# First gate's vectors moved out of the start, three scales summed on VectorE, adaLN loads issued from GpSimd's queue

## The chip, the cores and the metric

The kernel runs on one core of one Trainium2 chip. The metric is the device time of the whole program in microseconds (us), from the launch of its first instruction to its last. The kernel before took 2820.3 us, the median of three runs (2819.34 to 2823.11).

In the profile the engines are PE (TensorE's matmuls), PEld (TensorE's weight loads), DVE (VectorE), ACT (ScalarE), POOL (GpSimd) and SP (SyncE, which only issues DMAs). A name with q, as SPq, is the engine's sequencer, where DMA issues and waits stand. L250 is line 250 of the kernel.

## The reference, cut to what matters

Two layers over 512 latent and 256 context tokens of width 1024. A layer is a half-step SwiGLU of width 2816, a token mixer (layer 0: differential attention, layer 1: windowed attention with grouped queries), and a second half-step SwiGLU. Each of the three sub-layers is normalised, then shifted and scaled, and its result goes through a gate. These nine vectors of 1024 (shift, scale, gate, three times) come from one product per layer (adaLN):

```python
mod_l = silu(c) @ ada_w[i] + ada_b[i]         # for latent tokens
mod_c = silu(c_ctx) @ ada_w[i] + ada_b[i]     # for context tokens
sh1, sc1, g1, sh2, sc2, g2, sh3, sc3, g3 = split(mod_l, 9)
x = x + 0.5 * g1 * swiglu(rms(x) * (1 + sc1) + sh1, pre_wi, pre_wo)
```

`ada_w` is 1024 x 9216 float32 per layer. Everything is float32; the large products are done as three products of split operands (hi x hi, lo x hi, hi x lo).

## The kernel before, in words

**Layout.** `x` stays on the chip, features on the 128 partitions in 8 chunks (k or d, 0 to 7), 768 tokens along a row. An adaLN vector m (0 to 8; m = 0 is the first shift, 1 the first scale, 2 the first gate) has 8 chunks too, for the two types of token.

**How an adaLN vector is made.** There are three ways. `vector_job(m, k)` loads a row block of 128 x 1024 of `ada_w` (512 KB, tag `araw`, nine buffers) and multiplies it on VectorE with the replicated `crep = silu(c)`, once per type, each product summing along its row (L190); then it adds the bias (L191) and, for m = 2, halves it (L193). `scale_job(k)` makes chunk k of the scale on TensorE: eight pairs of small matmuls against `cvec` (L205), a turn (L209), and the bias plus 1 on VectorE (L211). `Halves` does the same as `vector_job` in half rows: a job loads 128 x 512 (256 KB, tag `wh`, three buffers), two products on VectorE (L250), and after eight chunks GpSimd adds the sums to `mod`, which already holds the bias (L229, L227), in L254; two halves q make a vector, and m = 2 or 8 is halved at the end (L256). One step is one job; `beside` runs steps after the up step of each f of the FFN, none up to f = 3 and one per f from there, `between` runs 13 of 16 (or 10) blocks' worth inside each down step.

**The start.** The 22 f of the FFN are 128 columns each of gate and up. f = 0 is fed: `feed(k)` normalises chunk k (L1156), applies shift and scale on ScalarE (L1159), splits it into `h_h` (L1160) and `h_l` (L1161), and TensorE multiplies that chunk at once (L537). `feed(k)` also issues the loads of the vector job m = 0 and the scale job of chunk k + 2 and runs the sums made ready two chunks earlier. After up(0), `beside(0)` runs the eight vector jobs of m = 2 and then releases the pool `start`. f = 1 and 2 are plain (L537) and f = 1 also makes the sums for the fast form; from f = 3 on `Seven.up` (L470) does an up step with seven products in place of eight. After f = 4, 8, ... a down step follows (L584), whose results go through the gate into `x` on VectorE (L396); the first of these needs vector m = 2 complete.

**What sets the order.** The program is written in one order; a planner simulates the engines and queues and orders each engine's instructions, so that work may move ahead of its place where its inputs are there. What is marked `keep` stays in program order on its queue. Nearly all loads stand in SP's queue: weights (`raw`, three buffers, L97), and the kept loads of `ada_w` (L184, L247) and of c (L236). An engine and a queue work in order: a load that waits for its buffer holds up what stands behind it.

**On GpSimd.** It adds squares for the next norm during the last down step and the output projection (L343), takes powers (L300, L627), does part of the attention's rotation (L648, L651), and the sums of adaLN (L254).

Of the kernel before, what the change touches and what calls it, by code (L numbers as in the profile page):

```python
# [12 lines left out]
ALU = mybir.AluOpType  # L13
# [4 lines left out]
P = 128  # L18
D = 1024
KC = D // P  # L20
# [11 lines left out]
def halves_of(nt):  # L32

    return [(0, SEQ, 0, (0, 1)), (SEQ, CTX, 1, (2,))] if nt == T else parts_of(nt)
# [8 lines left out]
def hybrid_backbone_kernel(ctx: ExitStack, tc: tile.TileContext, I, out):  # L43
    nc = tc.nc
# [9 lines left out]
    def one(name, tag="one"):  # L54
        return ps1.tile([P, 512], F32, name=name, tag=tag)
# [14 lines left out]
    keep = tc.keep_in_program_order  # L70
# [53 lines left out]
    adab = const.tile([P, 2, NMOD * KC], F32, name="adab")  # L124
# [56 lines left out]
    def vector_job(m, k, pool, crep, bufs):  # L181

        w = pool.tile([P, D], F32, name="araw", tag="araw", bufs=bufs)
        keep(nc.sync.dma_start(w, I["ada_w"][0, m * KC + k]))  # L184
        md = mods[0][m][2][:, :, k]

        def sums():
            for ty in range(2):
                o = w if ty else pool.tile([P, D], BF16, name="junk", tag="junk", bufs=2)
                nc.vector.scalar_tensor_tensor(o, w, 1.0, crep[:, ty], ALU.mult, ALU.mult, accum_out=md[:, ty:ty + 1])  # L190
            nc.vector.tensor_add(md, md, adab[:, 0, m * KC + k:m * KC + k + 1].broadcast_to([P, 2]))  # L191
            if m == 2:
                nc.vector.tensor_scalar_mul(md, md, 0.5)  # L193
        return sums

    def scale_job(k, pool, bufs):


        w = pool.tile([P, D], F32, name="araw", tag="araw", bufs=bufs)
        keep(nc.sync.dma_start(w, I["ada_s"][k]))  # L200

        def sums():
            ps = one("ps_a", "acc")
            for i in range(KC):
                nc.tensor.matmul(ps[:2, :P], cvec[:, i], w[:, i * P:(i + 1) * P], start=i == 0, stop=i == KC - 1)  # L205
            row = pool.tile([2, P], F32, name="row", tag="row", bufs=2)
            nc.scalar.copy(row, ps[:2, :P])
            pt = one("ps_b", "acc")[:, :2]
            nc.tensor.matmul(pt, row, ident[:2, :2], start=True, stop=True)  # L209
            bias = adab[:, 0, KC + k:KC + k + 1].broadcast_to([P, 2])  # L210
            nc.vector.scalar_tensor_tensor(mods[0][1][2][:, :, k], pt, 1.0, bias, ALU.add, ALU.add)  # L211
        return sums

    class Halves:
# [6 lines left out]
        def add(self, l, ms):  # L221
            def bias(m):
                md = const.tile([P, 2, KC], F32, name=f"mod{l}_{m}")
                mods[l][m] = md[:, 0], md[:, 1], md
                b = adab[:, l, m * KC:(m + 1) * KC].unsqueeze(1).broadcast_to([P, 2, KC])
                if m in (1, 4, 7):
                    nc.gpsimd.tensor_scalar_add(md, b, 1.0)  # L227
                else:
                    nc.gpsimd.tensor_copy(md, b)  # L229

            def silu(room, q):
                cs = []
                for nm in ("c", "c_ctx"):
                    pool, tag, bufs = (small, "ar", 3) if room[1] == "wh" else room
                    t = pool.tile([P, 512], F32, name="ch", tag=tag, bufs=bufs)
                    keep(nc.sync.dma_start(t, I[nm][q * 512:(q + 1) * 512].partition_broadcast(P)))  # L236
                    nc.scalar.activation(t, t, AF.Silu)
                    cs.append(t)
                self.c = cs

            def job(room, q, m, d):
                types = (0, 1) if l == 0 or m < 5 else (0,)
                if d == 0:
                    self.part = small.tile([P, 2, KC], F32, name="part", tag="part", bufs=2)
                pool, tag, bufs = room
                w = pool.tile([P, 512], F32, name="wh", tag=tag, bufs=bufs)
                keep(nc.sync.dma_start(w, I["ada_w"][l, m * KC + d, :, q * 512:(q + 1) * 512]))  # L247
                for ty in types:
                    o = w if ty == types[-1] else small.tile([P, 512], BF16, name="junkh", tag="tmp", bufs=4)
                    nc.vector.scalar_tensor_tensor(o, w, 1.0, self.c[ty], ALU.mult, ALU.mult,  # L250
                                                   accum_out=self.part[:, ty, d:d + 1])
                if d == KC - 1:
                    md, n = mods[l][m][2], len(types)
                    nc.gpsimd.tensor_add(md[:, :n], md[:, :n], self.part[:, :n])  # L254
                    if q == 1 and m in (2, 8):
                        nc.gpsimd.tensor_scalar_mul(md[:, :n], md[:, :n], 0.5)  # L256

            for q in range(2):
                for m in ms:
                    for d in range(KC):  # L260
                        def f(room, q=q, m=m, d=d):
                            if q == 0 and d == 0:
                                bias(m)
                            if m == ms[0] and d == 0:
                                silu(room, q)
                            job(room, q, m, d)
                        self.steps.append(f)
# [842 lines left out]
        return box["o"]  # L1110

    all_ = halves_of(T)
    FIRST = 9
    halves = Halves()
    h0 = Norm(0, 0, T, "right", "h0_")
    h0.open()
# [1 line left out]
    start = start_cm.__enter__()  # L1118
    cvec = start.tile([P, KC, 2], F32, name="cvec")
    nc.sync.dma_start(cvec, I["cvec"])  # L1120
    nc.scalar.activation(cvec, cvec, AF.Silu)
    for m in range(3):
        md = const.tile([P, 2, KC], F32, name=f"mod0_{m}")
        mods[0][m] = md[:, 0], md[:, 1], md
    with tc.tile_pool(name="f0", bufs=1) as pool:
        load_small()
        load_x(all_[0])
        crep = ada_vectors(start)
        load_x(all_[1])
        keep(nc.sync.dma_start(adab, I["ada_b"]))  # L1130
        first = [(vector_job(0, k, start, crep, FIRST), scale_job(k, start, FIRST)) for k in range(2)]
        xr = [pool.tile([P, T], F32, name="xr", tag=("ah", "al")[d % 2], bufs=5) for d in range(KC)]
        rall = pool.tile([P, T], F32, name="rall", tag="ah", bufs=5)
        steps = []
        for s0, n, _, _ in all_:
            tk = slice(s0, s0 + n)
            for d in range(KC):
                nc.scalar.activation(xr[d][:, s0:s0 + n], x[:, d, s0:s0 + n], AF.Square)
            for step in (1, 2, 4):
                for d in range(0, KC, 2 * step):  # L1140
                    nc.vector.tensor_add(xr[d][:, s0:s0 + n], xr[d][:, s0:s0 + n], xr[d + step][:, s0:s0 + n])
            steps.append(rstd_steps(xr[0][:, tk], n, D, lambda pr, _, tk=tk: nc.scalar.copy(rall[:, tk], pr), pool))
        for z in zip(*steps):
            for step in z:
                step()
        for z in first:
            for f in z:
                f()
        later = {}

        def feed(k):

            if k + 2 < KC:
                later[k + 2] = [vector_job(0, k + 2, start, crep, FIRST), scale_job(k + 2, start, FIRST)]
            hi, lo = h0.reg.hi[:, k], h0.reg.lo[:, k]
            nc.vector.tensor_mul(xr[k], x[:, k], rall)  # L1156
            for s0, n, ty, _ in all_:
                sh, sc = (mods[0][i][ty][:, k:k + 1] for i in range(2))
                nc.scalar.activation(xr[k][:, s0:s0 + n], xr[k][:, s0:s0 + n], AF.Identity, bias=sh, scale=sc)  # L1159
            nc.scalar.copy(hi, xr[k])  # L1160
            nc.vector.tensor_sub(lo, xr[k], hi.bitcast(F32))  # L1161
            for f in later.get(k + 2, ()):
                f()
        h1 = Norm(0, 3, T, "right", "h1_")

        def up_done():
            h0.reg.close()
            h1.open()
        halves.add(0, range(3, NMOD - 1))
        others = halves.beside(3)  # L1170

        def beside(f, seven):
            if f == 0:
                for k in range(KC):
                    vector_job(2, k, start, crep, FIRST)()
                start_cm.__exit__(None, None, None)
            else:
                if f == 17:
                    load_gains(0, "a")
                    load_rest(small)  # L1180
                if f < NF - 1:
                    others(f, seven)
        ffn(0, 0, I["pre_wi"][0], I["pre_wo"][0], T, h0, pool, up_done, h1.follow, "right", beside, halves.between(13), feed, xr)
# [125 lines left out]
```

## Time and profile before

| | |
|---|---|
| median of 3 runs | 2820.3 us (2819.34 to 2823.11) |
| the profiled execution: time, span | 2823.49 us, 2821.3 us |
| granted TensorE clock, mean | 0.988 |
| TensorE, VectorE, ScalarE, GpSimd busy | 96%, 77%, 43%, 12% |
| HBM read | 256 MB, 93 GB/s over the span |

The span is the time from the first to the last instruction of one profiled execution; its parts are read against its own time. A busy share is a mean over stages with different limits. The granted clock is the share of full TensorE speed; below 1 the engine ran part of the stretch at the lower of its two levels.

### The profile page before, as it was taken

How to read it: one execution, taken by the hardware profiler on the slowest of the kernel's cores; microseconds unless marked ns; L12 is line 12 of the kernel's file. 1: busy time of each engine (PE TensorE's matmuls, PEld its weight loads, DVE VectorE, ACT ScalarE, POOL GpSimd, SP SyncE). 2: the span in 40 equal slices, each digit the busy share in tenths (PEclk: the TensorE clock that was granted, in tenths of full speed). 3: DMA queues.
4: the chain of work that ended last, by engine and by line, in shares of the span. 5: the costliest groups of instructions: out<-in, count | busy, mean ns of one | idle time of the engine just before them, and what ended most of it. 6: DMA issues, size and time to landing. Idle time of an engine off the chain costs nothing. (4 is left out here: it accounts for less than half of the span.)

```text
span 2821.3 us, 47391 instructions
## 1 busy us (share of the span) xinstructions
PE 2705.1 (96%) x18028; PEld 2565.6 (91%) x18028; DVE 2176.2 (77%) x4703; ACT 1205.7 (43%) x2995; POOL 339.3 (12%) x464
## 2 busy tenths in 40 slices
PE   6899999999999899999999999999999999999999
PEld 4799998899999878999899989999999999999999
DVE  8788887876867768877787697777777766588887
ACT  4433332355656644333233352333235666444443
POOL 1000000034533421000000100000003421100000
PEclk9999999999999999999999999999999999999999
DMA  7234433321101142332333223433332101233232
GB/s 278 82 109 127 138 98 111 107 105 46 31 31 31 42 134 63 120 113 78 116 120 102 63 64 124 135 123 95 124 115 93 46 16 38 68 98 100 96 98 97
DMA packets 97555, 266.48 MB, mean 94 GB/s; under 512 B 12464, under 2 KB 16560, under 8 KB 97200
## 3 DMA queue, kind: packets, MB, share of 16 engines
q1 hardware_dynamic: 90816, 251.78, 27.6%
q10 hardware_dynamic: 6512, 11.68, 1.3%
q8 instruction: 142, 2.33, 0.3%
q14 instruction: 85, 0.70, 0.1%
HBM read 256.07 MB, written 7.34 MB: 93 GB/s over the span
## 5 line engine op out<-in xcount | busy, mean ns | idle before, releaser
L73 ACT CAST whi<-raw 128x512 fp32r<-128x512 f32 x548 | 336.1, 620 | 650.6 <-PE ps_dn L584 291.8
L584 PE MATMUL ps_dn<-ah,whi 128*128 128x256 f32 (+1 forms) x1456 | 464.9, 322 | 11.7 <-DVE x L396 9.5
L584 PE MATMUL ps_dn<-al,whi 128*128 128x256 f32 (+1 forms) x1456 | 462.2, 320 | 0.1
L584 PE MATMUL ps_dn<-ah,wlo 128*128 128x256 f32 (+1 forms) x1456 | 455.1, 319 | 1.1 <-DVE wlo L74 1.0
L74 DVE TENSOR_TENSOR wlo<-raw,whi 128x512 fp32r<-128x512 f32 x548 | 378.2, 695 | 65.5 <-ACT whi L73 49.9
L470 PE MATMUL ps_up<-h_h,whi 128*128 128x384 f32 (+1 forms) x1216 | 394.6, 325 | 8.3 <-DVE u L497 6.3
L470 PE MATMUL ps_up<-h_h,wlo 128*128 128x384 f32 (+1 forms) x1216 | 392.2, 324 | 0.7 <-DVE wlo L74 0.7
L470 PE MATMUL ps_up<-h_l,whi 128*128 128x384 f32 (+1 forms) x1216 | 392.5, 323 | 0.0
L396 DVE SCALAR_TENSOR_TENSOR x<-ps_dn,mod,x 128x256 f32<-128x256 f32 (+1 forms) x442 | 241.0, 556 | 126.6 <-PE ps_dn L584 103.0
L584 PEld LDWEIGHTS ps_dn<-ah,whi 128*128 128x128 f32 x1456 | 276.6, 191 | 35.8 <-ACT whi L73 8.5
L73 ACT CAST whi<-s 128x512 fp32r<-128x512 f32 x304 | 188.3, 620 | 266.6 <-PE ps_up L470 220.4
L584 PEld LDWEIGHTS ps_dn<-ah,wlo 128*128 128x128 f32 x1456 | 276.4, 191 | 21.8 <-DVE wlo L74 2.0
L584 PEld LDWEIGHTS ps_dn<-al,whi 128*128 128x128 f32 x1456 | 277.8, 191 | 19.6 <-DVE al L74 0.3
L470 PEld LDWEIGHTS ps_up<-h_h,whi 128*128 128x128 f32 x1216 | 229.0, 188 | 14.0 <-DVE u L497 8.9
L74 DVE TENSOR_TENSOR wlo<-s,whi 128x512 fp32r<-128x512 f32 x304 | 208.5, 687 | 31.4 <-ACT whi L73 27.7
L470 PEld LDWEIGHTS ps_up<-h_h,wlo 128*128 128x128 f32 x1216 | 228.3, 188 | 2.8 <-DVE wlo L74 2.3
L470 PEld LDWEIGHTS ps_up<-h_l,whi 128*128 128x128 f32 x1216 | 228.9, 188 | 0.5
L254 POOL TENSOR_TENSOR mod<-mod,part 128x16 f32<-128x16 f32 (+1 forms) x30 | 13.2, 439 | 1428.6 <-DVE wh L250 1428.6
L673 PE MATMUL ps_qkv<-whi,h_h 128*128 128x256 f32 x608 | 177.8, 292 | 3.2 <-DVE a L629 2.2
L250 DVE SCALAR_TENSOR_TENSOR wh<-wh,ch 128x512 f32<-128x512 f32 x240 | 163.4, 693 | 18.3 <-DMA wh<-in_ada_w 18.2
L673 PE MATMUL ps_qkv<-wlo,h_h 128*128 128x256 f32 x608 | 174.1, 286 | 0.7 <-DVE wlo L74 0.7
L673 PE MATMUL ps_qkv<-whi,h_l 128*128 128x256 f32 x608 | 173.6, 286 | 0.0
(236 smaller groups left out, 6536.5 us busy)
## 6 DMA issues: line engine op xcount, KB each, us to landing
wh<-in_ada_w SPq DMA_DIRECT2D x240, 256.0 KB, 3.8
raw<-in_pre_wi SPq DMA_DIRECT2D x88, 512.0 KB, 3.5
raw<-in_post_wi SPq DMA_DIRECT2D x88, 512.0 KB, 3.5
raw<-in_pre_wo SPq DMA_DIRECT2D x44, 512.0 KB, 3.6
raw<-in_post_wo SPq DMA_DIRECT2D x44, 512.0 KB, 3.6
araw<-in_ada_w SPq DMA_DIRECT2D x16, 512.0 KB, 4.4
raw<-in_a_w_qk SPq DMA_DIRECT2D x16, 512.0 KB, 3.5
araw<-in_ada_s SPq DMA_DIRECT2D x8, 512.0 KB, 10.0
```

Source lines behind the costliest of these rows:

```text
L73: nc.scalar.copy(hi, src)
L74: nc.vector.tensor_sub(lo, src, hi.bitcast(F32))
L250: nc.vector.scalar_tensor_tensor(o, w, 1.0, self.c[ty], ALU.mult, ALU.mult, accum_out=self.part[:, ty, d:d + 1])
L254: nc.gpsimd.tensor_add(md[:, :n], md[:, :n], self.part[:, :n])
L396: nc.vector.scalar_tensor_tensor(x[:, d, s0:s0 + n], ps, gate[ty][:, d:d + 1], x[:, d, s0:s0 + n], ALU.mult, ALU.add)
L470: nc.tensor.matmul(ps, ww, z[:, k, :n], start=first and k == 0 and i == 0, stop=k == 3 and i == 2, skip_group_check=True)
L584: nc.tensor.matmul(ps, wv, a[:, s0:s0 + n], start=fi == 0 and k == 0, stop=fi == nf - 1 and k == 2)
L673: nc.tensor.matmul(ps, h[:, k, bt], w, start=n == 0, stop=n == 23)
```

## The change

The vector jobs of m = 2 leave `beside(0)`. The gate's vector becomes the first member of `Halves` (16 steps, with c's two vectors loaded again for it), and `beside` runs 0, 4 and 12 steps after up(1), up(2) and up(3). Of the eight scale chunks, k = 5, 6, 7 are made by `vector_job(1, k)` in place of `scale_job`. The loads of `Halves` (`wh` and `ch`, in both layers) are issued from GpSimd's queue, not SP's.

```diff
-            nc.vector.tensor_add(md, md, adab[:, 0, m * KC + k:m * KC + k + 1].broadcast_to([P, 2]))
-            if m == 2:
-                nc.vector.tensor_scalar_mul(md, md, 0.5)
+            bias = adab[:, 0, m * KC + k:m * KC + k + 1].broadcast_to([P, 2])
+            if m:
+                nc.vector.scalar_tensor_tensor(md, md, 1.0, bias, ALU.add, ALU.add)
+            else:
+                nc.vector.tensor_add(md, md, bias)
...
-                    keep(nc.sync.dma_start(t, I[nm][q * 512:(q + 1) * 512].partition_broadcast(P)))
+                    keep(nc.gpsimd.dma_start(t, I[nm][q * 512:(q + 1) * 512].partition_broadcast(P)))
...
-                keep(nc.sync.dma_start(w, I["ada_w"][l, m * KC + d, :, q * 512:(q + 1) * 512]))
+                keep(nc.gpsimd.dma_start(w, I["ada_w"][l, m * KC + d, :, q * 512:(q + 1) * 512]))
...
-    FIRST = 9
+    FIRST, ONPE = 9, 5
...
-    for m in range(3):
+    for m in range(2):
...
-                later[k + 2] = [vector_job(0, k + 2, start, crep, FIRST), scale_job(k + 2, start, FIRST)]
+                later[k + 2] = [vector_job(0, k + 2, start, crep, FIRST),
+                                scale_job(k + 2, start, FIRST) if k + 2 < ONPE else
+                                vector_job(1, k + 2, start, crep, FIRST)]
...
+        halves.add(0, (2,))
         halves.add(0, range(3, NMOD - 1))
-        others = halves.beside(3)
+        others = halves.beside(3, (0, 4, 12))
...
             if f == 0:
-                for k in range(KC):
-                    vector_job(2, k, start, crep, FIRST)()
                 start_cm.__exit__(None, None, None)
```

## Rows read from the trace of the kernel before

**Rows 1.** The page, part 1: busy time (share of the span) x instructions.
```profile
PE 2705.1 (96%) x18028; PEld 2565.6 (91%) x18028; DVE 2176.2 (77%) x4703; ACT 1205.7 (43%) x2995; POOL 339.3 (12%) x464
```
**Rows 2.** Windows: stretch, length, busy per engine (x instructions), clock, DMA share, GB/s.
```profile
35.00:81.00 46.00, 30.57 (x179) 22.82 (x176) 46.00 (x101) 18.05 (x32) 0.00 (x0) 0.93 0.44 155
81.00:102.00 21.00, 20.29 (x97) 17.14 (x98) 18.30 (x37) 9.74 (x21) 0.00 (x0) 0.83 0.25 76
102.00:119.00 17.00, 17.00 (x99) 14.80 (x98) 7.00 (x13) 5.68 (x12) 0.00 (x0) 1.00 0.09 31
119.00:156.00 37.00, 36.25 (x206) 35.00 (x205) 33.03 (x79) 14.27 (x28) 0.53 (x1) 1.00 0.53 172
```
**Rows 3.** Timeline of TensorE: start, duration, what, count [idle before <- releaser].
```profile
74.11 0.28 PE L537 MATMUL ps_up<-h_h,wlo 128*128 128x256 f32 x1
80.92 0.79 PE L537 MATMUL ps_up<-h_h,whi 128*128 128x512 f32 x1 [6.54 <-ACT whi L73]
...
101.84 0.39 PE L537 MATMUL ps_up<-h_h,whi 128*128 128x512 f32 x1
...
118.73 0.34 PE L470 MATMUL ps_up<-h_h,whi 128*128 128x384 f32 x1
```
**Rows 4.** Timeline of VectorE, 71 to 77 us.
```profile
71.71 0.95 DVE L1161 TENSOR_TENSOR h_l<-xr,h_h 128x768 fp32r<-128x768 f32 x1
...
76.30 0.68 DVE L570 TENSOR_TENSOR sg<-sg,ps_up 128x512 f32<-128x512 f32 x1
```
**Rows 5.** Timeline of ScalarE, 73 to 81 us.
```profile
73.48 1.09 ACT L569 ACTIVATE sg<-ps_up 128x512 f32<-128x512 f32 x2 [5.28 <-PE ps_up L537]
77.01 0.62 ACT L73 CAST ah<-sg 128x512 fp32r<-128x512 f32 x1 [2.44 <-DVE sg L570]
...
80.25 1.14 ACT L73 CAST whi<-raw 128x512 fp32r<-128x512 f32 x2
```
**Rows 6.** Groups by line, 0 to 200 us: count | busy, mean ns | idle before.
```profile
L205 PE MATMUL ps_a<-araw,cvec 128*2 128x128 f32 x128 | 20.4, 326 | 6.5 <-DVE mod L211 3.8 <-DMA araw<-in_ada_s 2.8
L190 DVE SCALAR_TENSOR_TENSOR junk<-araw,crep 128x1024 bf16<-128x1024 f32 x16 | 19.5, 1218 | 0.0
```
**Rows 7.** Timeline of VectorE, 127 to 157 us.
```profile
127.22 0.69 DVE L250 SCALAR_TENSOR_TENSOR junkh<-wh,ch 128x512 bf16<-128x512 f32 x1
...
150.49 0.69 DVE L250 SCALAR_TENSOR_TENSOR wh<-wh,ch 128x512 f32<-128x512 f32 x1
...
151.10 0.69 DVE L250 SCALAR_TENSOR_TENSOR wh<-wh,ch 128x512 f32<-128x512 f32 x1
...
156.04 0.75 DVE L396 SCALAR_TENSOR_TENSOR x<-ps_dn,mod,x 128x512 f32<-128x512 f32 x1
```
**Rows 8.** Windows of L190 alone: VectorE busy (x instructions, reads of the accumulator counted), clock, DMA.
```profile
35.00:72.70 37.70, 27.33 (x47) 0.95 0.53 189
72.70:81.00 8.30, 4.70 (x8) 0.82 0.00 0
```
**Rows 9.** Waits of TensorE, 95 to 420 us: us in total, times, longest.
```profile
PE ps_dn L584 <- DVE x L396: 3.2, 1, 3.2
PE ps_dn L584 <- DVE wlo L74: 0.7, 1, 0.7
PE ps_up L470 <- DVE u L491: 0.4, 2, 0.2
```
**Rows 10.** Waits of GpSimd, whole span.
```profile
POOL mod L254 <- DVE wh L250: 1428.6, 30, 124.0
```
**Rows 11.** DMA issues: queue, count, KB each, median us to landing.
```profile
wh<-in_ada_w SPq DMA_DIRECT2D x240, 256.0 KB, 3.8
```
**Rows 12.** Waits of VectorE, whole span.
```profile
DVE s L456 <- DMA raw<-in_pre_wi: 38.4, 31, 2.9
...
DVE wh L250 <- DMA wh<-in_ada_w: 18.2, 18, 2.3
...
DVE junkh L250 <- DMA wh<-in_ada_w: 16.4, 19, 1.9
```

## The prediction

> **What bounds the kernel now.** First I read the page's busy shares: TensorE is busy 96% of the span [rows 1]. So only TensorE's idle stretches can be won, about 116 us in all (2821.3 minus 2705.1), and most of the change must be judged by whether it touches one of them. The table of windows then shows where they lie near the edit [rows 2]: from 35 to 81 us TensorE is busy 30.57 of 46.00 us while VectorE is busy for all 46.00. The start is bound by VectorE. From 81 to 102 us TensorE is busy nearly throughout but its granted clock is 0.83; from 102 us on it is busy at full clock, and VectorE has room (7.00 of 17.00 us, then 33.03 of 37.00). The waits of TensorE from 95 to 420 us say the same: all three together are 4.3 us, none of them for a DMA [rows 9]. So the pre-FFN of layer 0 is bound by VectorE up to 81 us and by TensorE afterwards.
>
> How the start ends is read in order of time. VectorE finishes the last `h_l` (L1161) at 72.66 us [rows 4], TensorE's last product of f=0 stands at 74.11 us, and the first of f=1 at 80.92 us, after 6.54 us idle put down to the cast of `whi` on ScalarE [rows 3]. ScalarE had taken the two SiLUs at 73.48, then waited 2.44 us for VectorE's `sg`, and only cast `whi` at 80.25 [rows 5]. VectorE delivered `sg` (L570) at 76.30 us, because it was still summing gate vectors [rows 4].
>
> **The change, part by part.** *Gate vectors leave the start.* A product of L190 with its read of the accumulator costs 1.18 us (4.70 us for the four pairs from 72.7 to 81 us, [rows 8]). In 35 to 81 us stand 27.33 + 4.70 = 32.03 us of them, so 27 of the 32 that the program has (16 for the first vector, 16 for the gate; the count is x16 for each of the two shapes, the first of them in [rows 6]). Five were done before. Left are therefore 11 products of the first vector, and the edit adds two for each of k = 5, 6, 7 of the scale, 6 in all. Of the 23 products that now lie ahead of the last `h_l`, 17 remain: 6 x 1.18 = 7.1 us less VectorE time before it. The bounds are 0 (if the loads and ScalarE set the pace at once) and 7.1 us; I take 6, near the upper end, since VectorE has no idle time there at all [rows 2], less about 1 us because the last product must still pass through ScalarE before the last `h_l`.
>
> *Three scales move from TensorE to VectorE.* The 6 products above are their price. On TensorE the 128 matmuls of L205 are 20.4 us for eight chunks [rows 6], 2.55 us each, so 7.7 us is freed; TensorE has 15.4 us idle in that stretch [rows 2], so I cost this at nothing. The cover is VectorE being later than TensorE; without it the 7.7 us would be a gain on top.
>
> *The passage from f=0 to f=1.* Four more gate products, the x8 of [rows 8], vanish from beside `sg`. If ScalarE keeps its order (SiLU, `ah`, `whi`), `sg` can follow the SiLU at 74.6 on the old time scale instead of at 76.30, and both casts of `ah` then run one after the other; `whi` comes at about 76.4 in place of 80.25, a gain of 3.9 us. If `whi` is cast right after the SiLU, the gain is 5.7. I take 4.5. What is late next is the release of f=0's `whi` buffers by TensorE, which no edit touches.
>
> *The clock.* f=2 takes 118.73 - 101.84 = 16.89 us, f=1 101.84 - 80.92 = 20.92 us for the same 96 matmuls [rows 3], and the granted clock is 0.83 over f=1 [rows 2], so part of it ran at 1.2 instead of 2.4 GHz, after TensorE had stood idle for 6.54 us. With a gap of 1 to 3 us the 4.0 us may come back wholly, partly or not at all; I take 2, the middle.
>
> *The gate comes back in f=2 and f=3.* 16 half rows, two products each of 0.61 us (150.49 to 151.10 us to the next, [rows 7]): 19.5 us of VectorE, needed before the first `x` of the down step, now at 156.04 us [rows 7]. VectorE's idle time from 81 to 156 us is 2.7 + 10.0 + 4.0 = 16.7 us [rows 2], and in that stretch some eleven half rows of later vectors are already done ahead of that `x`, the first at 127.22 us [rows 7]; they carry no date there and can slide behind. So the cost is between nothing and 19.5 - 4.0 = 15.5 us (if only the idle time behind 119 us can be used, because the gate's half rows are issued behind up(2) and up(3)). I take 2, near the lower end, because the first half rows now are done some 30 us ahead of their place in the program.
>
> *Loads from GpSimd's queue.* 256 issues (16 of them the silu vectors' loads) leave SP's queue, and 16 for the gate join them on GpSimd's. TensorE waits for no weight load in [rows 9], so SP's relief is worth nothing by itself; VectorE's 38.4 us until `raw` [rows 12] is idle time of an engine that has some. On GpSimd the loads stand in one queue with the sums `mod` (L254), which wait for the last product of a vector [rows 10]: behind each of 32 such sums the next vector's first load goes out late. No row shows a load issued by GpSimd. From [rows 11] one lands 3.8 us after its issue from SP. Bounds: a gain of 4 us (all the waits of [rows 9]) and, per sum, a loss of 3.8 us less what TensorE has in hand. A half slab feeds 12 matmuls of 0.176 us (16.89 / 96), 2.1 us; that leaves 1.7 us for each of 32, 54 us at most. I take 0, as the row it is nearest to is VectorE's waiting for these loads now, 18.2 + 16.4 us over the two shapes of L250 [rows 12], of which TensorE's 4.3 us show no trace.
>
> A rule speaks against this part. The large VectorE instructions of this stretch take two inputs and all run at one pace (512 columns in 0.69 us, 1024 in 1.22 us, [rows 6, 7]); none shows a doubled rate. The Trainium skill, page "SBUF — State Buffer", section "SBUF: two separate sides", says that a DMA issued from GpSimd has its descriptors written by GpSimd's cores, and that these are locked out while VectorE runs an instruction that takes both ports. No such instruction stands among those rows, so by the rule, too, the sum is the one above; but it is a reason to keep the chance of late loads above nothing.
>
> *Sum.* 6 + 4.5 + 2 - 2 + 0 = 10.5 us less. The profiled execution's span was 2821.3 us and its time 2823.49, 2.2 us around it; the median of the runs is 2820.3, 3.2 us below. From span 2821.3 to 2810.8; the execution 2813.0; the median 2809.8, say 2810.
>
> **Rivals.** (a) *The gate takes it back.* VectorE becomes the bound in f=2 to f=4: with 15.5 us in place of 2 the sum is 12.5 - 15.5, so 2823. For it: VectorE is busy 33 of 37 us from 119 to 156. Against it: 10 us idle just before, and the eleven half rows that can slide. 0.12.
> (b) *Loads behind the sums on GpSimd's queue come late*, place: the 32 sums L254 from layer 0's pre-FFN to layer 1's; price 1.7 us each on TensorE once VectorE waits for a half row in front of a `wlo`. From 7 such places on it eats the gain (10.5 / 1.7 = 6.2), at half of them (16 x 1.7 = 27 us) the time is 2837, at all 2864. For it: 1428.6 us of GpSimd's idle time are spent ahead of exactly these sums [rows 10]. Against it: three buffers of `wh`, and much of that waiting lies where no vector is due soon. 0.13.
> (c) *SP's relief gains as well*: weights land earlier, VectorE's 38.4 us until `raw` shrinks, the clock's 4 us come back wholly. 2 + 3 us more: 2805. For it: VectorE is at 80 to 90% beside TensorE's work. Against it: [rows 9] names no load. 0.11.
> (d) *The start does not get shorter as reckoned*, because the scales' six products or the loads set the pace; then only the passage is won, 4.5 - 2 = 2.5 us: 2818. For it: the scales put 7.1 us on the engine that is the bound. Against it: 12 gate products leave the same place. 0.07.
> The forecast has 0.57.
>
> **How the numbers follow.** The time is the forecast's, 2810. What this kernel's measurement can tell from no change is about 0.2%, 5.6 us: faster is under 2814.7, slower over 2825.9. Faster: the forecast but for a little (0.55) and (c), 0.66. Same: the rest of the forecast, (d) and most of (a), 0.17. Slower: (b) and the tail of (a), 0.17. The range reaches down to 2802 (passage 5.7, start 7.1, clock 4.0, with 1 us of (c)) and up to 2824 so that it holds (d) and most of (a), and leaves out (b).
>
> **What would show it.** In the profile after: the last `h_l` at 65 to 68 us; the first product of f=1 at 69 to 72 us with under 3 us idle before it; granted clock over f=1 above 0.9; first `x` of the down step at 142 to 148 us; L250 products from 85 us on; TensorE's waits from 95 to 420 us still a few us. Wrong would be: `x` (L396) later than 150 us (then (a)), or waits of VectorE for `wh` well over the 34.6 us of now, with TensorE waiting for `wlo` behind them (then (b)).

## The result, and the profile after

The changed kernel takes 2868.03 us (median of 4 runs, 2864.5 to 2870.53), the kernel before beside it 2821.49 us: a ratio of 1.0158, 95% interval [1.0145, 1.0171]. It is 46.5 us slower where 10 us faster was forecast. Two single executions of later runs, one of the six with the gate alone and one of the eight with the split 2, 6, 8, took 5406 and 5280 us, and the ratios leave them out. In the program after, the lines behind L190 stand two further on (L1161 four, as L1165): the products of the half rows are L252 (before L250), their loads L249, the sums into `mod` L256, the up step of the fast form L472, the down step L586, `x` L398.

The start went as forecast. From VectorE's timeline the last `h_l` and the first `x` of the down step, 4.3 and 8.4 us ahead of [rows 4, 7]:

```profile
67.37 0.95 DVE L1165 TENSOR_TENSOR h_l<-xr,h_h 128x768 fp32r<-128x768 f32 x1
...
147.65 0.74 DVE L398 SCALAR_TENSOR_TENSOR x<-ps_dn,mod,x 128x512 f32<-128x512 f32 x1
```

In TensorE's timeline the last product of f=0 and the first of f=1 follow each other with no idle time in brackets; before, 6.54 us stood here [rows 3]:

```profile
69.77 0.29 PE L539 MATMUL ps_up<-h_h,wlo 128*128 128x256 f32 x1
69.90 0.40 PE L539 MATMUL ps_up<-h_h,whi 128*128 128x512 f32 x1
```

Two of the prediction's signs did not come: the products of half rows begin at 70.85 us and not at 85, and TensorE's waits from 95 to 420 us, 4.3 us before [rows 9], are 20.5 us.

The windows answer to [rows 2] with its columns (stretch, length, PE, PEld, DVE, ACT, POOL busy, clock, DMA share, GB/s). The first four are its stretches, the last three lie further on:

```profile
35.00:81.00 46.00, 36.52 (x183) 29.28 (x182) 46.00 (x94) 25.14 (x45) 2.28 (x4) 0.89 0.34 117
81.00:102.00 21.00, 21.00 (x119) 18.16 (x119) 19.91 (x48) 6.21 (x13) 2.78 (x6) 1.00 0.32 102
102.00:119.00 17.00, 14.18 (x84) 13.86 (x83) 13.80 (x31) 8.58 (x18) 4.52 (x9) 0.97 0.52 163
119.00:156.00 37.00, 34.95 (x190) 32.34 (x190) 33.49 (x83) 11.47 (x21) 6.73 (x14) 0.97 0.53 167
160.00:260.00 100.00, 91.81 (x514) 86.38 (x513) 94.75 (x230) 30.61 (x55) 20.04 (x39) 0.98 0.46 146
1100.00:1200.00 100.00, 80.91 (x469) 74.41 (x469) 95.61 (x228) 38.31 (x78) 16.94 (x32) 0.91 0.37 118
1700.00:1800.00 100.00, 89.18 (x487) 82.07 (x486) 87.14 (x205) 30.02 (x57) 26.21 (x50) 0.95 0.50 163
```

The last three of before:

```profile
160.00:260.00 100.00, 99.85 (x572) 94.30 (x571) 87.14 (x193) 32.70 (x59) 0.76 (x2) 1.00 0.37 118
1100.00:1200.00 100.00, 97.53 (x573) 89.58 (x572) 90.32 (x190) 41.24 (x81) 0.22 (x1) 1.00 0.31 101
1700.00:1800.00 100.00, 99.36 (x564) 94.14 (x563) 78.74 (x166) 33.74 (x63) 1.19 (x2) 1.00 0.38 122
```

From 81 to 102 us TensorE is fully busy at full clock (before 0.83). What is lost is lost later: 8, 17 and 10 us of TensorE in the last three windows, while VectorE is busier than before. They lie in the early up and down steps of layer 0's first FFN, of its second one, and of layer 1's first. The page and the waits of VectorE and GpSimd (us in total, times, longest) show whether the half rows came late:

```profile
PE 2710.9 (95%) x17974; PEld 2575.9 (90%) x17974; DVE 2191.6 (76%) x4731; ACT 1206.8 (42%) x2996; POOL 483.3 (17%) x744
...
L249 POOL DMA_DIRECT2D wh<-in_ada_w x256 | 138.7, 543 | 684.0 <-DVE wh L252 633.8
...
wh<-in_ada_w POOLq DMA_DIRECT2D x256, 256.0 KB, 3.3
```
```profile
POOL wh L249 <- DVE wh L252: 633.8, 162, 163.6
POOL mod L256 <- DVE wh L252: 146.1, 30, 10.0
...
DVE junkh L252 <- DMA wh<-in_ada_w: 18.4, 19, 2.3
...
DVE wh L252 <- DMA wh<-in_ada_w: 10.0, 11, 4.4
```

They did not. VectorE waits 28.4 us for `wh` in all, less than the 34.6 us of [rows 12]. GpSimd's loads wait almost only for VectorE to empty a buffer of `wh`. The sums wait 146.1 us where they waited 1428.6 [rows 10], but much of that has only changed its place: GpSimd now spends 684.0 us idle ahead of the loads, in the same stream. The products of the half rows alone (DVE busy, clock, DMA share, GB/s), after and then before:

```profile
60.00:160.00 100.00, 32.50 (x96) 0.97 0.43 137
160.00:260.00 100.00, 42.79 (x128) 0.98 0.46 146
260.00:360.00 100.00, 33.82 (x100) 0.97 0.41 137
360.00:460.00 100.00, 0.00 (x0) 1.00 0.21 70
```
```profile
60.00:160.00 100.00, 15.24 (x46) 0.95 0.33 109
160.00:260.00 100.00, 26.24 (x78) 1.00 0.37 118
260.00:360.00 100.00, 24.15 (x72) 1.00 0.36 117
360.00:460.00 100.00, 21.49 (x64) 1.00 0.34 110
```

Before, the half rows were spread evenly, from 160 us on at 21 to 26 us in 100. After, they crowd into the first 300 us of the FFN and are used up by 360 us.

The costliest place shows how that stops TensorE. First windows of all engines (columns as above), then of L252 alone:

```profile
1120.00:1140.00 20.00, 19.77 (x111) 17.14 (x110) 20.00 (x45) 6.57 (x13) 2.68 (x5) 1.00 0.43 132
1140.00:1160.00 20.00, 14.54 (x90) 13.04 (x88) 20.00 (x49) 8.12 (x18) 3.11 (x6) 0.97 0.33 105
1160.00:1180.00 20.00, 10.18 (x42) 10.16 (x43) 19.70 (x50) 5.95 (x11) 4.85 (x9) 0.60 0.41 132
```
```profile
1120.00:1140.00 20.00, 6.67 (x20) 1.00 0.43 132
1140.00:1160.00 20.00, 6.71 (x20) 0.97 0.33 105
1160.00:1180.00 20.00, 9.94 (x30) 0.60 0.41 132
```

VectorE has no idle time from 1120 to 1160 us; 13.4 of the 40 us are products of half rows, for vectors of later stages. Timelines of VectorE, then ScalarE, then TensorE at the end of it (start, duration, what, [idle before <- releaser]):

```profile
1162.30 0.68 DVE L458 TENSOR_TENSOR s<-raw 128x512 f32<-128x512 f32 x1
1162.91 0.68 DVE L252 SCALAR_TENSOR_TENSOR wh<-wh,ch 128x512 f32<-128x512 f32 x1
...
1165.54 0.68 DVE L459 TENSOR_TENSOR s<-s,raw 128x512 f32<-128x512 f32 x1
1166.14 0.68 DVE L252 SCALAR_TENSOR_TENSOR junkh<-wh,ch 128x512 bf16<-128x512 f32 x1
...
1166.75 0.68 DVE L460 TENSOR_TENSOR s<-raw 128x512 f32<-128x512 f32 x1
...
1167.82 0.68 DVE L252 SCALAR_TENSOR_TENSOR junkh<-wh,ch 128x512 bf16<-128x512 f32 x1
...
1168.43 0.68 DVE L461 TENSOR_TENSOR s<-raw,s 128x512 f32<-128x512 f32 x1
```
```profile
1169.15 0.62 ACT L73 CAST whi<-s 128x512 fp32r<-128x512 f32 x1 [4.54 <-DVE s L461]
```
```profile
1169.82 0.69 PE L472 MATMUL ps_up<-h_h,whi 128*128 128x384 f32 x1 [15.28 <-ACT whi L73]
```

TensorE's wait reads "for ScalarE". ScalarE had nothing to do for 4.54 us, because the sums `s` of the fast form's weights came one by one from VectorE, with a product of a half row between each pair. Eight such products, some 5.4 us, stand in TensorE's 15.28 us of idleness; that the rest of it is work that had piled up behind the earlier ones is argued and not shown. The granted clock from 1160 to 1180 us, with the end of the 15.28 us of idleness in it, is 0.60.

### The profile page after: what moved, and what is told of

It reads as the page before. It is cut to its first block, busy times and chain, and to the rows that moved or that the text cites. A ratio compares the mean times of both kernels' runs of the same rounds, so it can differ in the third digit from the quotient of the medians.

```text
span 2866.0 us, 47437 instructions
## 1 busy us (share of the span) xinstructions
PE 2710.9 (95%) x17974; PEld 2575.9 (90%) x17974; DVE 2191.6 (76%) x4731; ACT 1206.8 (42%) x2996; POOL 483.3 (17%) x744
## 4 chain that ended last, share of the span: by engine, by line
PE 73%; DVE 12%; issue 5%; DMA 4%; ACT 3%; POOL 3%; SPq 0%; ACTq 0%; POOLq 0%; DVEq 0%
PE ps_up L472 28%; PE ps_dn L586 21%; PE ps_qkv L675 8%; PE ps_up L539 4%; PE ps_dn L752 3%; DVE wlo L74 2%; PE ps_av L1021 2%; DMA wh<-in_ada_w 2%; DVE wh L252 1%; DVE junkh L252 1%; PE ps_av L854 1%; PE ps_s L810 1%; PE ps_qkvs L688 1%; PE ps_pt L1010 1%; DMA raw<-in_pre_wi 1%
## 5 line engine op out<-in xcount | busy, mean ns | idle before, releaser
L586 PE MATMUL ps_dn<-ah,whi 128*128 128x256 f32 (+1 forms) x1456 | 464.3, 322 | 11.3 <-DVE x L398 9.0
L586 PE MATMUL ps_dn<-al,whi 128*128 128x256 f32 (+1 forms) x1456 | 462.5, 320 | 0.1
L586 PE MATMUL ps_dn<-ah,wlo 128*128 128x256 f32 (+1 forms) x1456 | 454.0, 319 | 2.0 <-DVE wlo L74 2.0
L472 PE MATMUL ps_up<-h_h,whi 128*128 128x384 f32 (+1 forms) x1216 | 399.7, 329 | 25.4 <-ACT whi L73 20.4
L472 PE MATMUL ps_up<-h_l,whi 128*128 128x384 f32 (+1 forms) x1216 | 397.7, 327 | 0.0
L472 PE MATMUL ps_up<-h_h,wlo 128*128 128x384 f32 (+1 forms) x1216 | 395.8, 327 | 1.6 <-DVE wlo L74 1.6
L398 DVE SCALAR_TENSOR_TENSOR x<-ps_dn,mod,x 128x256 f32<-128x256 f32 (+1 forms) x442 | 241.1, 555 | 120.6 <-PE ps_dn L586 99.4
L586 PEld LDWEIGHTS ps_dn<-ah,whi 128*128 128x128 f32 x1456 | 276.8, 191 | 34.1 <-ACT whi L73 9.8
L586 PEld LDWEIGHTS ps_dn<-ah,wlo 128*128 128x128 f32 x1456 | 276.2, 191 | 22.4 <-DVE wlo L74 2.6
L586 PEld LDWEIGHTS ps_dn<-al,whi 128*128 128x128 f32 x1456 | 278.0, 191 | 19.8 <-DVE al L74 0.3
L472 PEld LDWEIGHTS ps_up<-h_h,whi 128*128 128x128 f32 x1216 | 233.0, 192 | 30.2 <-ACT whi L73 21.2
L249 POOL DMA_DIRECT2D wh<-in_ada_w x256 | 138.7, 543 | 684.0 <-DVE wh L252 633.8
L472 PEld LDWEIGHTS ps_up<-h_h,wlo 128*128 128x128 f32 x1216 | 232.5, 191 | 3.0 <-DVE wlo L74 2.9
L472 PEld LDWEIGHTS ps_up<-h_l,whi 128*128 128x128 f32 x1216 | 233.0, 192 | 0.3
L74 DVE TENSOR_TENSOR wlo<-s,whi 128x512 fp32r<-128x512 f32 x304 | 208.0, 686 | 32.1 <-ACT whi L73 27.6
L345 POOL TENSOR_TENSOR ar<-ar,sq 128x256 f32<-128x256 f32 x84 | 66.1, 792 | 706.9 <-ACT sq L343 704.7
L252 DVE SCALAR_TENSOR_TENSOR wh<-wh,ch 128x512 f32<-128x512 f32 x256 | 175.1, 690 | 10.5 <-DMA wh<-in_ada_w 10.0
```

Source lines behind the costliest of these rows:

```text
L74: nc.vector.tensor_sub(lo, src, hi.bitcast(F32))
L249: keep(nc.gpsimd.dma_start(w, I["ada_w"][l, m * KC + d, :, q * 512:(q + 1) * 512]))
L345: add(self.acc[p], self.acc[p], sq)
L398: nc.vector.scalar_tensor_tensor(x[:, d, s0:s0 + n], ps, gate[ty][:, d:d + 1], x[:, d, s0:s0 + n], ALU.mult, ALU.add)
L472: nc.tensor.matmul(ps, ww, z[:, k, :n], start=first and k == 0 and i == 0, stop=k == 3 and i == 2, skip_group_check=True)
L586: nc.tensor.matmul(ps, wv, a[:, s0:s0 + n], start=fi == 0 and k == 0, stop=fi == nf - 1 and k == 2)
```

## The experiments

Each ran in three rounds beside the kernel before on the same chip; every time is a median, and ratios are to the kernel before. Three theories stood. **G**: the gate and the scales cost, VectorE being the bound where they now run. **S**: a load issued by GpSimd costs as such (late, slow, or it disturbs VectorE). **P**, pacing: in SP's queue these loads stand behind weight loads that wait for buffers, and so go out at TensorE's pace; in a queue without the weights nothing holds them, the planner puts half rows far ahead of their place, and they crowd VectorE where it has the most to do.

**The two halves of the change alone.** The change with the loads on SP:

```diff
-                keep(nc.gpsimd.dma_start(w, I["ada_w"][l, m * KC + d, :, q * 512:(q + 1) * 512]))
+                keep(nc.sync.dma_start(w, I["ada_w"][l, m * KC + d, :, q * 512:(q + 1) * 512]))
```
(and `ch` likewise).

> The gate's vectors later and the three scales on VectorE, as in the change, but all adaLN loads in SP's queue as before. Theory P (pacing: in SP's queue the loads of wh stand behind weight loads that wait for their buffers, so the half rows come at the pace of TensorE; in GpSimd's queue nothing holds them back and VectorE is filled with them ahead of the weight splits): the part of the prediction about the start holds, 2806 to 2818 us; by the evictions of x, the first at 144 to 149 us and the lead of 5 to 13 us kept to the end. Theory G (the gate's 16 half rows in f = 2 and 3 and the scales on VectorE are what costs): 2850 us or more. Theory S (loads issued by GpSimd are themselves late or slow VectorE): 2806 to 2818 us as well.

Measured: 2810.35 us, ratio 0.9965 [0.9953, 0.9978], with the first `x` at 142.04 us, a little ahead of what was expected. S had expected the same time, so this run speaks against G alone. And the queue alone, that edit the other way round in the kernel before:

> The kernel before with only the loads of wh and ch moved to GpSimd's queue. Theory P: 2855 to 2885 us, with VectorE over 90% busy after each start of a batch of adaLN vectors (120 to 300, 1100 to 1300 and 1680 to 1800 us) and its products of wh over 35 us per 100 us there, in place of 26 us. Theory G: 2820 us, no change. Theory S: 2855 us or more too, but with VectorE waiting for wh well over the 35 us of before.

Measured: 2870.96 us, ratio 1.0178 [1.0163, 1.0194]. VectorE waits 26.9 us for `wh` there, not over 35 as S had expected, and the products of half rows take 35.5 us from 1100 to 1200 us, as P had. So G falls: the gate and scales gain 11 us by themselves. The queue alone costs 49.6 us (2870.96 less 2821.39), and 57.7 us on top of the rest (2868.03 less 2810.35).

**The gate alone, loads on SP.** `FIRST, ONPE = 9, 8`: all eight scale chunks on TensorE.

> The gate's vectors later, all eight scales on TensorE as before, all adaLN loads in SP's queue. Theory P with the start bound by VectorE: six products of 1.18 us fewer on VectorE than in the run with the three scales there, so the last h_l comes up to 7 us earlier, if TensorE's 7.7 us for the three chunks stay hidden; time 2 to 8 us below that run: 2800 to 2814 us. If TensorE is by now as late as VectorE in the start, equal to that run within 2 us.

Measured: 2813.54 us, ratio 0.9965 [0.9951, 0.9978], the same ratio as with the three scales on VectorE. The gain did not come, and the second case did: the last `h_l` stands at 67.4 us in its trace, against 65.64 us with the three scales on VectorE. From 35 to 70 us VectorE waits 3.8 us for scales from TensorE, so TensorE was now the later of the two.

**The weights moved instead.** To part P from S: in the kernel before, `raw` is issued by GpSimd and `wh` stays on SP, now without the weights.

```diff
-        i = nc.sync.dma_start(raw, src)
+        i = nc.gpsimd.dma_start(raw, src)
```

> The kernel before with the two kinds of load parted the other way: the weights (raw) are issued from GpSimd's queue, wh and ch stay in SP's queue, alone there. No adaLN load is issued by GpSimd. Theory P (in a queue without the weights nothing paces the half rows): they bunch as in the run with the queue alone, over 50 products of L250 from 150 to 250 us (67 there, 43 before), and the time is 2850 us or more. Theory S (it is GpSimd that issues them): no bunching, under 45 products in that stretch, and whatever the weights lose by being issued there, with TensorE's waits naming raw. The time alone does not tell the two apart, the bunching does.

Measured: 2888.71 us, ratio 1.0235 [1.0216, 1.0254]; 67 products of half rows from 150 to 250 us. (The expectation misquotes a count: in the run with the queue alone that stretch has 55, in the kernel before 41.) The half rows crowd as after the change although SP issues them. That speaks for P and against S, but it doesn't settle the matter, as the weights came from GpSimd's queue here.

**One buffer of `wh`.** `(seven.pool, "wh", 1)` in place of 3 in the changed kernel.

> The changed kernel, loads in GpSimd's queue, but one buffer of wh in place of three, so that a load can only go out when the half row before it is summed. Theory P: this paces the half rows (one per 0.55 us of issue + 3.3 us to land + 1.4 us of products + the wait for its turn, 6 us or so, in place of 3 us), so VectorE is less crowded: most of the loss comes back, 2815 to 2845 us. Theory S: every half row now waits for its own load, VectorE's waits for wh grow to 100 us and more and the time rises over 2880 us. Theory G: 2868 us, no change or worse.

Measured: 2912.62 us, ratio 1.0325 [1.0308, 1.0342]; P's number was missed, and both of S's came: a time over 2880 us, and 163.9 + 60.0 us of VectorE's waits for `wh`. From 608 to 656 us the half rows come one by one, each after its own load, ahead of the attention's norm, and one wait of TensorE for that norm is 48.2 us. With one buffer each load must wait for the product before it; how much of this SP's queue would show as well was not tried, so the run doesn't part the theories.

**The half rows in the weights' buffers**, on either queue, in the kernel before (the run on SP leaves the second edit out):

```diff
-                w = pool.tile([P, 512], F32, name="wh", tag=tag, bufs=bufs)
-                keep(nc.sync.dma_start(w, I["ada_w"][l, m * KC + d, :, q * 512:(q + 1) * 512]))
+                w = wp.tile([P, 1024], F32, name="raw", tag="raw", bufs=3)[:, :512]
+                keep(nc.gpsimd.dma_start(w, I["ada_w"][l, m * KC + d, :, q * 512:(q + 1) * 512]))
```

> The kernel before with wh and ch in GpSimd's queue and each wh tile taken from the three buffers of raw in their rotation, so that a half row's load waits for the weight slab before it to be split: the pace comes from a buffer, not from a queue. To be read against the next run, which differs from it in the queue alone. Theory P: within 12 us of the next run, and its L250 products from 150 to 250 us between 35 and 50. Theory S: 35 us or more above the next run.

> The kernel before with each wh tile taken from the three buffers of raw in their rotation, all loads in SP's queue. It gives the level for the run before it: the weights lose prefetch, so 2820 to 2860 us under both theories.

Measured: 2906.16 us on GpSimd's queue, 1.0296 [1.0276, 1.0316], and 2890.32 us on SP's, 1.0238 [1.022, 1.0256]. Sharing the buffers is dear in itself (SP's run lies 30 us above its expected range). Once they are shared, the queue makes 16 us and not 50. That is under S's 35, and above P's 12; the 36 products from 150 to 250 us on GpSimd's queue are within P's 35 to 50.

**Half of the crowd's work.** The first of each half row's two products is left out (where a vector has both types, one type's sums are not made, nor added to `mod`), on either queue:

```diff
-                for ty in types:
+                for ty in types[-1:]:
```

> The changed kernel, loads of wh and ch in GpSimd's queue, but of the two products of a half row only the last is done: the sums for the other type of token are left out, so its vectors hold the bias alone. Read against the next run, which differs from it in the queue alone. The loads and their queue are as in the changed kernel; only VectorE's time in the half rows is halved, from about 1.4 to 0.7 us each. Theory P (VectorE crowded by half rows that come in a bunch): the loss by the queue, 57 us between the changed kernel and the run with gate and scales on SP's queue, falls to half or less, 5 to 30 us. Theory S (the loads by GpSimd as such): 45 us or more remain.

> The gate later and three scales on VectorE with all loads in SP's queue, the sums for one type of token left out of each half row: the level for the run before it. VectorE is not the bound beside TensorE in the FFN, so little is gained by leaving them out: 2795 to 2812 us under both theories.

Measured: 2846.82 us, 1.01 [1.0085, 1.0115], on GpSimd's queue and 2798.23 us, 0.9931 [0.991, 0.9952], on SP's. The difference is 48.6 us. P had expected 5 to 30 and S 45 or more, so by its time the run came out as S had it. A count in the traces says why. I counted the products on VectorE between two results `x`: from the 113th to the 129th (the start of layer 0's second FFN) and from the 224th to the 241st (the start of layer 1's first).

```
                              113th to 129th   224th to 241st
kernel before                       32               23
change, loads on SP                 32               23
changed kernel                      80               60
queue alone                         79               60
weights from GpSimd                 80               67
one product each, GpSimd's queue    53               54
one product each, SP's queue        12               15
```

With one product each, the planner pulled forward more half rows, and as much work: 41 and 39 products more than on SP, 28 and 27 us at 0.69 us each; the two stretches are 20 and 22 us longer. In the changed kernel the surplus over the loads on SP is 48 and 37 products, 33 and 26 us, and the stretches are 27.6 and 20.7 us longer. Of that 15.2 and 12.7 us are idle time of TensorE; in the rest it is busy for longer, at a granted clock of 0.91 and 0.94 over the two stretches, where the run on SP has 0.96 and 0.99. So leaving work out didn't take the crowd away.

**Pacing given back to GpSimd's queue.** The direct test: the changed kernel with `wh` taken from the rotation that the up steps' sums `t` and `s` use, so that a load waits for an up step; then the same on SP's queue.

```diff
-                    self(early[i - 1] if i <= len(early) else int(i > first), (seven.pool, "wh", 3))
+                    self(early[i - 1] if i <= len(early) else int(i > first), (seven.pool, "s", 7))
...
-            s1, s2, s3, s4 = (self.pool.tile([P, 512], F32, name="s", tag="s", bufs=4) for _ in range(4))
+            s1, s2, s3, s4 = (self.pool.tile([P, 512], F32, name="s", tag="s", bufs=7) for _ in range(4))
```
(`between` and the three `t` likewise; `ch` keeps its own buffers).

> The changed kernel with loads on GpSimd's queue as they are, but wh takes its tiles from the rotation that the up steps' sums s and t use (seven buffers in one rotation, in place of four and three), so a load can start only when an up step's tiles ahead of it are free. Pacing (half rows run ahead because nothing holds their loads): with this hold the half rows follow the up steps again, 150 to 250 us has 47 to 55 products of wh and not 69, and the time is 2805 to 2830. A cost of loads issued by GpSimd as such: nothing comes back, 2860 or more.

> The control: the same shared rotation of seven, loads on SP's queue. Both theories: near the change with SP loads, 2805 to 2825. Pacing: within 10 us of the run with GpSimd's queue. Cost of the loads as such: at least 40 us below it.

Measured: 2836.61 us, 1.0058 [1.0041, 1.0075], on GpSimd's queue, and 2821.32 us, 0.9997 [0.9986, 1.0008], on SP's. Windows of the half rows' products alone, from 1100 to 1200 us: changed kernel, this one on GpSimd's queue, this one on SP's, and the kernel before:

```profile
1100.00:1200.00 100.00, 34.38 (x103) 0.91 0.37 118
```
```profile
1100.00:1200.00 100.00, 16.04 (x48) 1.00 0.30 98
```
```profile
1100.00:1200.00 100.00, 16.34 (x48) 1.00 0.32 103
```
```profile
1100.00:1200.00 100.00, 16.17 (x48) 1.00 0.31 101
```

And all engines there in the run on GpSimd's queue:

```profile
1100.00:1200.00 100.00, 98.25 (x580) 89.97 (x580) 92.50 (x197) 41.37 (x83) 7.58 (x14) 1.00 0.30 98
```

The crowd is gone (38 and 23 products in the table's two stretches, 44 from 150 to 250 us), TensorE is busy 98.25 us where it was 80.91, and 31.4 us come back although the loads are still GpSimd's. The two queues now differ by 15.3 us, where it was 57.7. S is refuted for that part. P's numbers were missed by some us, though: the time lies above 2830, and the two queues were to be within 10 us; with the weights' buffers 16 remained as well. Where the rest stands can be read from the two traces (profiled executions of 2835.75 and 2814.5 us, the second the fastest of its ten): 5.6 us at the first `x` (152.57 against 146.92 us), and 10.5 us in the table's first stretch (141.3 against 130.8 us), with 38 products against 32. In this run GpSimd's loads wait in its own stream (the next row; us in total, times, longest), and what GpSimd computes stands behind them; whether that is the cause was not tried.

```profile
POOL wh L249 <- DVE wlo L74: 812.1, 88, 47.9
```

One rival within P stays open. VectorE's order is laid down by the planner before the program runs, and moving a load to another queue changes what the planner may do. No run kept VectorE's order and moved the queue alone, so it isn't shown how much of the crowd the queue itself lets in on the chip, and how much is the planner's choice.

**Other splits of the gate, loads on SP.** `halves.beside(3, (2, 6, 8))` and `(4, 6, 6)` in place of `(0, 4, 12)`.

> The gate later and three scales on VectorE, all loads in SP's queue, and the gate's 16 half rows spread 2, 6 and 8 behind up(1), up(2) and up(3) in place of 0, 4 and 12. If the planner's place in the program sets when they are summed, VectorE's room at 102 to 119 us is used better and the first eviction of x comes 1 to 4 us sooner than in the run with 0, 4, 12: 2804 to 2812 us. If it moves them ahead anyway as its simulated loads allow, the same within 4 us.

> The gate later and three scales on VectorE, all loads in SP's queue, the gate's half rows 4, 6 and 6 behind up(1), up(2) and up(3). After 0, 4, 12 and 2, 6, 8, which came out alike, the same again is expected, 2805 to 2815 us; if the half rows behind up(1) get in the way of the sums of the fast form there, a few us more.

Measured: 2809.3 us, 0.9951 [0.9937, 0.9965], and 2813.11 us, 0.998 [0.9969, 0.999]. The first has the lowest median of all kernels here that compute everything, 0.4 to 0.6% below the kernel before; beside the change's own split on SP (0.9965) the intervals overlap. Its first `x` comes at 141.97 us, against 142.04 with 0, 4, 12, so the split made no difference there.

## Why the prediction was wrong

**The step that failed** is "Loads from GpSimd's queue", "I take 0, as the row it is nearest to is VectorE's waiting for these loads now". Alone it measured 49.6 us, and 57.7 us on top of the rest. That the first lies near the upper end of that step's own bounds ("54 us at most") is luck, as the mechanism behind that end did not occur. I had asked only whether a load could come late. What the move took away was the hold: SP issues its loads in order, so a half row's load went out when the weight loads ahead of it had found a buffer. The profile of before shows it in SP's waits, which the prediction doesn't use (us in total, times, longest), and in SP's timeline at the start of layer 0's second FFN:

```profile
SPq L97 <- DVE wlo L74: 1912.3, 261, 46.4
SPq L247 <- DVE wh L250: 130.1, 108, 5.3
```
```profile
1062.66 82.17 SPq L97 DMA_DIRECT2D raw<-in_post_wi  x9
```

SP waited 1912.3 us ahead of weight loads until VectorE had split a slab, and 130.1 us ahead of half rows for one of their own buffers. For 82 us, in the first up steps there, it issued nine weight loads and no half row; in the changed kernel GpSimd issues 13 half rows in those steps, from 1109 to 1154 us. The waits that I did quote don't show the hold. GpSimd's sums waited 1428.6 us [rows 10], but 225.4 us in the run with the shared sums, whose half rows are paced as well; VectorE's 34.6 us for `wh` [rows 12] are 22.7 us there. I took the 4.3 us of TensorE's waits [rows 9] as proof that the waiting for these loads did nothing. I had even counted eleven half rows done ahead of the first `x`, as work that "can slide behind"; that they would run ahead as soon as nothing held them was not among the rivals.

**Rival (b)** has the right step and sign, and its price at all places, 2864, is near the time measured, but by luck: its mechanism is wrong, "late" half rows, with VectorE's waits "well over the 34.6 us of now". They are 28.4 us. The half rows came too early, and TensorE waits not for a load but for sums and weight splits that VectorE does between them.

**The rule weighed in the prediction** does not carry the loss. The Trainium skill, page "SBUF — State Buffer", section "SBUF: two separate sides", would have GpSimd's descriptors wait while VectorE holds both ports. No run here shows it: a load lands 3.3 us after its issue from GpSimd, 3.8 us from SP [rows 11], and none of the 256 issues took over 0.65 us. As the prediction had found no instruction of that kind among its rows, this leaves the rule untested.

**What held.** With the loads on SP the other steps are tested by themselves: 2810.35 us against a forecast of 2810. From the timelines of that run (VectorE's last `h_l` and first `x`, TensorE's first product of f=1 and of f=2):

```profile
65.64 0.96 DVE L1165 TENSOR_TENSOR h_l<-xr,h_h 128x768 fp32r<-128x768 f32 x1
...
142.04 0.76 DVE L398 SCALAR_TENSOR_TENSOR x<-ps_dn,mod,x 128x512 f32<-128x512 f32 x1
```
```profile
68.33 0.40 PE L539 MATMUL ps_up<-h_h,whi 128*128 128x512 f32 x1
...
85.23 0.40 PE L539 MATMUL ps_up<-h_h,whi 128*128 128x512 f32 x1
```

- The gate's departure, taken at 6 us: the last `h_l` is 6.1 us earlier than [rows 4]; in the changed kernel 4.3 us.
- The passage, taken at 4.5 us: f=1 begins 12.6 us earlier than [rows 3], so the passage gave 6.5 us. In the changed kernel it begins at 69.90 us with no idle time, inside the 69 to 72 us expected.
- The clock, taken at 2 us: f=1 takes 16.90 us in place of 20.92, at a granted clock of 1.00, so all 4.0 us came back. A stretch at the lower level now stands ahead of it, in f=0: the clock is 0.50 from 55 to 62.7 us, while VectorE is busy throughout.
- The gate's return, taken at 2 us: f=3 begins 16.6 us earlier (102.10 us) and the first `x` 14.0 us, so it cost 2.6 us.
- The scales on VectorE: no difference to TensorE (2810.35 and 2813.54 us, equal ratios), as the term of nothing said.

So the mechanisms held, but that the sum is met to the us is partly luck: the lead at the first `x` is 14.0 us where 10.5 were forecast, and 11.1 us are left at the last `x`. No term of the prediction stands for the 3 us that go in between.

Rivals (a) and (d) would have shown with the loads on SP as 2823 and 2818 us; that run lies between 2806.31 and 2816.37, and the gate's return cost 2.6 us and not (a)'s 15.5. Rival (c)'s clock came back in full, but with the loads on SP, so not by SP's relief; nor did that show elsewhere: VectorE's wait for `raw` in the changed kernel is 35.5 us, 38.4 before [rows 12], and the move of the queue alone only lost.

## What to carry to other kernels

An in-order queue is also a throttle: before loads are moved out of it, ask what they wait behind there, and what the work that they feed will displace when they no longer wait. The issuing queue's own waits show what it holds back (here SP's 1912.3 us ahead of weight loads); the waits of the engine that uses the loads did not (34.6 us with the hold, 28.4 us without). If such loads need another queue, give them a hold of their own (here buffers that the stage itself sets free, which took the queue's price from 57.7 to 15.3 us), and judge the move by counting the work per stage, since the busy share of the whole span hardly moves (VectorE 77% before, 76% after).

## What the runs showed of the hardware

- A 256 KB load costs GpSimd 0.543 us to issue (138.7 us for 256), in its stream beside its arithmetic, and landed in 3.3 us (3.7 us in the run with the shared sums).
- A single idle stretch of TensorE of 15.28 us ends at 1169.82 us. From 1160 to 1180 us the granted clock is 0.60, so part of these 20 us stood at 1.2 in place of 2.4 GHz; products of 128x384 took 0.34 us each ahead of the idle stretch, and 0.53 us from 1170.30 to 1175.42 us.
- One product of 0.69 us too many on VectorE in a crowded stretch made the stretch 0.5 to 0.6 us longer (27.6 us for 48, 20.7 us for 37): most of its own length, in a kernel whose VectorE is idle for a quarter of the span.
